# Second FFN of a hybrid block: load order on SP, places of the downward steps, loads of the last weights

## The chip, the cores and the metric

The kernel runs on one core of one Trainium2 chip. The metric is the device time of one execution in microseconds (us). Lower is better. Times before are the median of three runs, and the profile is of one more execution.

## The reference, cut to what matters

One block: a first feed-forward layer, a mixer of retention and sparse attention, a second feed-forward layer and a last norm, over 16 meta tokens and 512 real ones, in fp32. The change touches the second feed-forward layer, which here works on the 512 real tokens alone.

```python
D_MODEL, SEQ, D_FF = 1024, 512, 2816

def swiglu(u, w_gate, w_up, w_down):
    return (jax.nn.silu(u @ w_gate) * (u @ w_up)) @ w_down

# second FFN and the end of the block
h = h + 0.5 * swiglu(rmsnorm(h, ffn2_norm[l]), ffn2_w_gate[l], ffn2_w_up[l], ffn2_w_down[l])
y = rmsnorm(h, final_norm)
return y[:, N_META:]
```

## The kernel before

**Arithmetic.** Every fp32 operand is used as a high and a low part: ACT writes the high part of a weight (`whi`), DVE subtracts it from the raw weight to get the low part (`wlo`), and TensorE (PE) does three matmuls for each product. Now and then the two parts go into one spare buffer and are both called `wpair`.

**Units and steps.** The 2816 hidden columns are cut into six units: `u0` of 256 columns, `u1` to `u5` of 512. A unit from `u1` on is done by seven block products of tokens and gate or up weights, in the order `11`, `12`, `b`, `a`, `c`, `d`, `22` (`11`, `12`, `22` are blocks of the weights, `a` to `d` are sums of blocks). Each product is two steps, so a unit has upward steps 0 to 13; a step is 12 matmuls. They go to the PSUM banks X (tag `x`) and Z or Y (both tag `z`); in a profile these are `psqX`, `psqZ`, `psqY`, line 2489. Step 0 of the next unit begins bank X anew, so it waits until DVE has read the old X (`gated("A", ...)`, line 2352, `p<-psqX,RR,p`). Step 6 begins Y in the bank of Z, so it waits until DVE has added Z to the first copy (`add("A", "Z")`, line 2343, `p<-psqZ,p`, after step 3).

**The way of the hidden values.** After step 12 the second token half is gated, and after step 13 the first half. DVE transposes each in blocks (line 2359, `cross`), POOL writes them to DRAM in four DMAs (line 2362, `hts<-cross`), and SP fetches them back turned (line 2369, `land<-hts`; for `u0` the lines are 2552, 2555 and 2558). In the next unit ACT and DVE split them, with their block sums, into `hh`, `hl` and `he` (`turned_sums`; `hidden` for `u0` and for `u5`).

**Downward steps.** The product with `w_down` of units 1 to 4 is again seven block products, here called d0 to d6, one step of 12 matmuls each (`sums_down`, `psd`, line 2462). Their banks are reused: d4 may begin when DVE has taken d2 out of its bank, d5 after d3, d6 after d4 (`take`, line 2452, `hTok<-psd,hTok`). The steps of unit i - 1 are woven between the steps of unit i. Units 0 and 5 have plain downward steps (`down`, line 2660, 24 matmuls each).

**What sets the order.** `steps` is one list, and `steps_through` runs through it. At step i it first issues the load of step i + 4 (`pre`), then puts the `whi` of step i + 2 or i + 3 on ACT, then the matmuls of step i; half way through them come the `wlo` on DVE (`lower`) and all work put off to `late` (`catch_up`), and after them the step's posts (`posts_of`), among them `next_place`, which loads the next 1 MB upward weight into one of four places, in two DMAs. PE, ACT and DVE work through this in the written order, which `manual_schedule(engines=BUSY)` says. Up to step 13 of `u5` SP is not in that set: the framework's scheduler places its DMAs. From there to the end SP is in written order as well.

Of the kernel before, what the change touches and what calls it, by code (L numbers as in the profile page):

```python
# [18 lines left out]
P = 128  # L19
D = 1024  # L20
KD = D // P
S = 512
# [59 lines left out]
def kernel(ctx: ExitStack, tc: tile.TileContext, x, meta, g1, wg1, wu1, wd1, gm,  # L82
                      w_in, w_ro, w_ao, w_mo, g2, wg2, wu2, wd2, gf, rope, decay, causal, out):
    nc = tc.nc
    x, out = x[0], out[0]
# [3 lines left out]
    wg2, wu2, wd2 = wg2[0], wu2[0], wd2[0]  # L89
# [26 lines left out]
    def split(src, hi, lo, eng=nc.vector):  # L116
        nc.scalar.activation(hi, src, AF.Copy)  # L117
        eng.tensor_tensor(lo, src, hi.bitcast(F32), ALU.subtract)  # L118
# [11 lines left out]
    def load_w(src, nk, n):  # L130
        raw = wpool.tile([P, 2048], F32, tag="raw", name="raw", bufs=2)
        v = raw[:, : nk * n].rearrange("p (k c) -> p k c", k=nk)
        nc.sync.dma_start(v, src.rearrange("(k p) c -> p k c", p=P))
        return v

    def split_w(v, eng=nc.vector):
        nk, n = v.shape[1], v.shape[2]
        hi = wpool.tile([P, 1024 + WPAD], F32R, tag="whi", name="whi", bufs=3)[:, w_at[0] :]
        lo = wpool.tile([P, 1024 + WPAD], F32R, tag="wlo", name="wlo", bufs=3)[:, w_at[0] :]
        hv = hi[:, : nk * n].rearrange("p (k c) -> p k c", k=nk)  # L140
        lv = lo[:, : nk * n].rearrange("p (k c) -> p k c", k=nk)
        split(v, hv, lv, eng)
        return hv, lv
# [234 lines left out]
    BUSY = {mybir.EngineType.PE, mybir.EngineType.Activation, mybir.EngineType.DVE}  # L378
# [261 lines left out]
    if True:  # L640
# [226 lines left out]
        with tc.manual_schedule(engines=BUSY):  # L867
# [9 lines left out]
            raw = load_w(wg1[:, 2 * P : 4 * P], KD, 2 * P)  # L877
# [17 lines left out]
            raw = load_w(wu1[:, 2 * P : 4 * P], KD, 2 * P)  # L895
# [18 lines left out]
        def down(f0, nf, taken_by):  # L914

            raws = {}
            steps = []
            for c in range(KD):
                def pre(c=c):
                    if c % 2 == 0:  # L920
                        raws[c] = load_w(wd1[f0 * P : (f0 + nf) * P, c * P : (c + 2) * P], nf, 2 * P)

                def src(c=c):
                    return raws[c // 2 * 2][:, :, c % 2 * P : (c % 2 + 1) * P]

                def run(w, lower, c=c):
                    ps = [s1.bank("psd")[:, :TH] for _ in range(2)]
                    mm3([(ps[0], one), (ps[1], two)], w, lambda k: s1.hid[f0 + k], nf)
                    lower()
                    s1.catch_up()  # L930
                    for p_, sl in zip(ps, (one, two)):
                        nc.vector.scalar_tensor_tensor(hT[c][:, sl], p_, 0.5, hT[c][:, sl], ALU.mult, ALU.add)
                    taken_by(c)
                    s1.next_sum4()

                steps.append((pre, src, run))
            return steps
# [13 lines left out]
        steps = down(0, 4, keep_sums)  # L951
# [332 lines left out]
        units = [Values(0, OFF_RV), Values(1, OFF_RV + 2 * S), Values(2, OFF_AV)]  # L1284
# [185 lines left out]
    if True:  # L1470
# [418 lines left out]
        p = RH - 1  # L1889
# [69 lines left out]
        raw = vr["raw"]  # L1959
# [3 lines left out]
        for c in range(2):  # L1963
            t = rt.tile([P, S], F32, tag="sg", name="gate", bufs=4)
# [18 lines left out]
    with pool("ao") as ao:  # L1983
        vo = [ao.tile([P, AH, S], F32R, tag=f"vo{i}", name="vo") for i in range(2)]
        ao_parts = [(vo[0][:, c, :], vo[1][:, c, :]) for c in range(AH)]
        with pool("at") as at:
# [39 lines left out]
            def rope_k(ps, eng=nc.gpsimd):  # L2026
                y = rope_swap(ps, cos, sin, 64, T, eng)
                k = [at.tile([P, TX], F32R, tag=f"ak{i}", name="ak")[:, :T] for i in range(2)]
                split(y, k[0], k[1])
                return k  # L2030
# [103 lines left out]
            with tc.manual_schedule(engines=BUSY):  # L2134
                w = gr.next()
                k, q = rope_k(first_k, nc.vector), rope_q(first_q, nc.vector)
                t, t5 = (at.tile([P, S], F32, tag="gate", name="gate", bufs=2) for _ in range(2))
# [10 lines left out]
                raw = fetch_values(5, vraw())  # L2148
            pend = None
            for h in range(AH):  # L2150
# [9 lines left out]
                if more:  # L2160
                    q, k = proj_q(w if h == 0 else None), proj_k()
# [40 lines left out]
        steps = []  # L2202
# [4 lines left out]
        with pool("ou") as ou:  # L2207
# [6 lines left out]
            for c in range(KD):  # L2214
# [3 lines left out]
                if c < n_left:  # L2218
                    t = ou.tile([P, S], F32, tag="sa", name="sa", bufs=3)
                    nc.scalar.dma_start(t, gd[KD + c])  # L2220
                else:
                    t = sa[c - n_left]
# [20 lines left out]
    late, f2, fin = [], {}, {}  # L2243
# [31 lines left out]
    def new_place(name):  # L2275
        return places.tile([P, 4, S], F32, tag="w", name=name, bufs=4)
# [283 lines left out]
    units = [(Plain, Rows)[i > 0](i, f0, nf) for i, (f0, nf) in enumerate(UNITS)]  # L2560
# [192 lines left out]
    def posts_of(u):  # L2753

        i = u.i
        nxt = units[i + 1] if i + 1 < len(units) else None
        prev = units[i - 1] if i else None
        at = {j: [] for j in range(14)}

        def put(j, *do):  # L2760
            at[j] += do

        gate_of = lambda c, half: lambda: u.silu(c, half)
        if u is u0:
            put(0, lambda: split_t(1), lambda: new_t(2))
            put(1, lambda: split_t(2), lambda: new_t(3), lambda: squares(0))
            put(2, lambda: split_t(3), lambda: new_t(4), lambda: squares(1), lambda: squares(2), lambda: squares(3), token_norm)
            put(3, load_gf, lambda: split_t(4), u.gates, lambda: u1.wsum("b", 0), lambda: late.append(u.turned))
            return at
        put(1, lambda: u.copy("A", "p1", "X"))  # L2770
        put(2, lambda: put_off and put_off.pop()())
        put(3, lambda: u.add("A", "Z"), lambda: late.append(gate_of("A", 0)))
        if u.early:
            put(4, lambda: prev.new_hidden(hid_tile), lambda: late.append(prev.hidden(1)))
            put(6, lambda: late.append(prev.hidden(0)))
            put(1, lambda: u.wsum("b", 2))
            put(6, lambda: u.wsum("d", 0))
            put(7, lambda: u.wsum("d", 2))
        else:
            sums = []  # L2780
            put(2, lambda: sums.extend(prev.turned_sums()), lambda: sums[0]())
            put(4, lambda: sums[1]())
            put(5, lambda: sums[2]())
            put(6, lambda: sums[3]())
            put(8, lambda: sums[4]())
        put(5, lambda: u.copy("B", "u2", "X"))
        put(7, lambda: u.copy("C", "p5", "Y"))
        put(9, lambda: u.add("C", "X"))
        put(11, lambda: u.add("B", "Y"), lambda: late.append(gate_of("B", 1)))
        put(12, lambda: u.gated("C", u.room["C"], u.room["B"], 1), lambda: u.turn("C", "D", 1), lambda: u.fetch("C", 1))  # L2790
        put(13, lambda: u.gated("A", u.d["X"], u.room["A"], 0), lambda: late.append(turn_rest))
        for j in ((5, 7, 9, 11, 13) if u.early else range(1, 14, 2)):
            put(j, next_place)

        def turn_rest():
            u.turn("A", "B", 0)
            u.fetch("D", 0)

        return at
# [4 lines left out]
    def woven(i, places_):  # L2804

        for j, s in enumerate(wo[i]):
            steps.append(s)
            if j in places_:
                steps.append(places_[j])
# [11 lines left out]
    def halves_of_raw(i):  # L2821

        if not down_raw:
            t = wpool.tile([P, 2048], F32, tag="raw", name="raw", bufs=2).rearrange("p (h k c) -> p h k c", h=2, k=2)
            down_raw.extend(t[:, j] for j in range(2))
        down_raw.append(down_raw.pop(0))
        return down_raw[-1]

    for i in (2, 3, 4):
        woven(i, dict(zip(range(6, 13), units[i - 1].sums_down(halves_of_raw, {}))))  # L2830
    u4, u5 = units[4:]

    tail_w = []
# [4 lines left out]
        for low in lows:  # L2838
            low()

    tail_raw = []

    def load_tail():
        tail_raw.append(new_place("raw"))
        nc.sync.dma_start(tail_raw[0], wd2[u5.f0 * P : (u5.f0 + 4) * P, S:].rearrange("(k p) c -> p k c", p=P))

    def tail_weights():
        tail_w.extend(split_w(tail_raw[0][:, i : i + 2, :]) for i in (0, 2))

    ends = {}  # L2850

    def halves_of_place(i):
        if i < 3:
            return halves_of_raw(i)
        j = (i - 3) // 2
        if j not in ends:
            ends[j] = new_place("raw")
        return ends[j][:, (i - 3) % 2 * 2 :][:, :2]

    d = u4.sums_down(halves_of_place, {4: (load_tail,), 6: (last_halves,)})  # L2860
    woven(5, {7: d[0], 9: d[1], 11: d[2]})
    n_units = len(steps)
    c0, c1 = [], []
    steps += d[3:]
    steps.append(down(u5, 0, 0, c0, posts=(tail_weights,), rows=(2, 3, 0, 1), where=("x", "z")))
    steps.append(down(u5, 0, 2, c0, taken_by=finish))
    pair = []

    def other_parts(n, c):
# [5 lines left out]
    for i in range(lead_from + 3, n_units - 2, 4):  # L2875
        steps[i] = (*steps[i], other_parts)
        lead_to[:] = [i]
    with tc.manual_schedule(engines=BUSY):
        for _ in range(n_units):
            next(pipe)  # L2880
    f2["later"].close()
# [7 lines left out]
    with tc.manual_schedule(engines=BUSY | {mybir.EngineType.SP}):  # L2889
        c1 += [new_bank(t) for t in LAST]  # L2890
        ends = [(c1[b], wide) for b in range(3)] + [(c1[3][:, one], one)]
# [58 lines left out]
```

## Time and profile before

| | |
|---|---|
| median of 3 runs | 1526.95 us (1525.93 to 1526.99) |
| the profiled execution | 1525.19 us, its span 1523.4 us |
| mean granted TensorE clock | 0.988 |
| PE busy | 1485.2 us, 97% of the span |
| DVE, ACT, POOL busy | 1133.4, 733.8, 241.2 us |
| second FFN | from 1162.8 us (its first split in the chain) to the end |

How to read it: a 128x512 matmul that follows another starts 0.23 us after it, so a step of 12 takes 2.72 us, which is the beat of this stage. A time inside the stage is told from the span's start, or as T + so many us, where T is the end of the step 13 that is spoken of. A window's row gives each engine's busy time in that stretch, the granted clock of TensorE (1.00 is full), the busy share of the DMA engines and GB/s. A row of waits gives the engine and its line, what ended the wait, the sum, the count and the longest.

### The profile page before, as it was taken

Reading aid. Unit: us, or ns where it says so; the run is one execution under the profiler, and the core shown is the slowest. Engines: PE = TensorE matmul, PEld = TensorE weight load, DVE = VectorE, ACT = ScalarE, POOL = GpSimd, SP = SyncE. Lnnn points to the kernel's source line nnn. Section 1 sums busy time; section 2 is a strip of 40 time slices with the busy share of each in tenths; the row PEclk is TensorE's granted clock in tenths of the full one; section 3 lists DMA queues with packets and bytes.
Section 4 is the critical chain, followed back from the end, with each engine's and each line's share of the span. In section 5 each row is a group of like instructions: output and inputs, shape, how many; then the busy total and the mean of one; then the engine's idle time right before and its main releaser. Section 6 shows DMA issues by size and latency. Waiting matters only on the chain.

```text
span 1523.4 us, 22754 instructions
## 1 busy us (share of the span) xinstructions
PE 1485.2 (97%) x8800; PEld 1312.6 (86%) x8800; DVE 1133.4 (74%) x1747; ACT 733.8 (48%) x1052; POOL 241.2 (16%) x335
## 2 busy tenths in 40 slices
PE   9999999999999999999999999999999989999996
PEld 8999999999988888888888888988888777777775
DVE  4988585776887768778887878775567669678685
ACT  5555263454354444443333366775345444545443
POOL 1001010013221231212121323221012010010110
PEclk9999999999999999999999999999999999999998
DMA  5266566568776677676766645566474455666622
GB/s 168 78 184 164 152 172 166 151 169 251 244 211 205 194 202 210 165 215 143 212 156 164 172 115 165 156 195 194 133 265 139 158 184 202 202 210 203 218 91 103
DMA packets 198300, 269.78 MB, mean 177 GB/s; under 512 B 17328, under 2 KB 120904, under 8 KB 197552
## 3 DMA queue, kind: packets, MB, share of 16 engines
q1 hardware_dynamic: 171184, 207.89, 42.8%
q0 software_dynamic: 23904, 54.92, 16.3%
q10 hardware_dynamic: 3104, 5.53, 1.1%
q8 instruction: 69, 1.13, 0.3%
q14 instruction: 39, 0.32, 0.1%
HBM read 238.12 MB, written 80.49 MB: 209 GB/s over the span
## 4 chain that ended last, share of the span: by engine, by line
PE 88%; DVE 5%; DMA 3%; ACT 2%; issue 2%; POOL 0%; SPq 0%; ACTq 0%; POOLq 0%; DVEq 0%
PE psd L157 8%; PE psqX L157 7%; PE psrg L157 6%; PE psro L157 6%; PE psqX L2489 5%; PE psvX L1234 4%; PE psd L2462 4%; PE psqY L157 3%; PE psrk L157 3%; PE psqY L2489 3%; PE psrq L157 3%; PE psat L157 3%; PE psmo L157 3%; PE psak L157 3%; PE psaq L157 3%; PE psga L157 3%
## 5 line engine op out<-in xcount | busy, mean ns | idle before, releaser
L375 ACT ACTIVATE whi<-raw 128x1024 fp32r<-128x1024 f32 (+2 forms) x167 | 159.5, 957 | 132.2 <-PE psd L157 33.6
L376 DVE TENSOR_TENSOR wlo<-raw,whi 128x1024 fp32r<-128x1024 f32 (+2 forms) x167 | 187.7, 1127 | 46.2 <-ACT whi L375 46.1
L376 DVE TENSOR_TENSOR wlo<-w,whi 128x1024 fp32r<-128x1024 f32 x58 | 70.3, 1218 | 30.2 <-ACT whi L375 29.9
L375 ACT ACTIVATE whi<-w 128x1024 fp32r<-128x1024 f32 x58 | 61.2, 1057 | 51.5 <-PE psqY L2489 12.6
L157 PE MATMUL psro<-vo,whi 128*128 128x512 f32 x256 | 78.8, 389 | 0.0
L157 PE MATMUL psd<-hl,whi 128*128 128x264 f32 x352 | 71.4, 284 | 0.0
L157 PE MATMUL psd<-hh,wlo 128*128 128x264 f32 x352 | 70.8, 283 | 0.0
L117 ACT ACTIVATE whi<-raw 128x1024 fp32r<-128x1024 f32 (+1 forms) x44 | 45.4, 1036 | 52.4 <-PE psat L157 17.2
L157 PE MATMUL psd<-hh,whi 128*128 128x264 f32 x352 | 70.6, 282 | 0.0
L118 DVE TENSOR_TENSOR wlo<-raw,whi 128x1024 fp32r<-128x1024 f32 (+1 forms) x44 | 53.7, 1221 | 22.0 <-ACT whi L117 21.9
L2362 POOL DMA_DIRECT2D hts<-cross x40 | 25.7, 650 | 270.2 <-DVE cross L2359 269.9
L157 PE MATMUL psqX<-th,whi 128*128 128x264 f32 x216 | 61.1, 283 | 0.0
L157 PE MATMUL psqX<-tl,whi 128*128 128x264 f32 x216 | 61.1, 283 | 0.0
L157 PE MATMUL psqX<-th,wlo 128*128 128x264 f32 x216 | 61.1, 283 | 0.0
L157 PEld LDWEIGHTS psro<-vo,whi 128*128 128x128 f32 x256 | 48.1, 188 | 10.1 <-DVE vo L376 0.2
L157 PEld LDWEIGHTS psd<-hh,wlo 128*128 128x128 f32 x352 | 54.6, 188 | 0.0
L157 PEld LDWEIGHTS psd<-hh,whi 128*128 128x128 f32 x352 | 54.2, 188 | 0.0
L157 PEld LDWEIGHTS psd<-hl,whi 128*128 128x128 f32 x352 | 53.8, 188 | 0.0
L375 ACT ACTIVATE whi<-wsum 128x1024 fp32r<-128x1024 f32 x36 | 38.1, 1059 | 30.4 <-PE psd L157 14.9
L157 PE MATMUL psrg<-xh,whi 128*128 128x512 f32 x128 | 50.5, 394 | 0.0
L157 PE MATMUL psrg<-xl,whi 128*128 128x512 f32 x128 | 49.9, 390 | 0.0
L157 PE MATMUL psrg<-xh,wlo 128*128 128x512 f32 x128 | 49.9, 390 | 0.0
(622 smaller groups left out, 4822.9 us busy)
## 6 DMA issues: line engine op xcount, KB each, us to landing
raw<-in_w_in_dram SPq DMA_DIRECT2D x18, 1024.0 KB, 6.3
raw<-in_w_in_dram SPq DMA_DIRECT2D x33, 512.0 KB, 4.5
w<-in_w_in_dram SPq DMA_DIRECT2D x24, 512.0 KB, 6.0
raw<-in_ffn_w_up_dram SPq DMA_DIRECT2D x11, 1024.0 KB, 5.4
raw<-in_ffn_w_gate_dram SPq DMA_DIRECT2D x10, 1024.0 KB, 5.6
raw<-in_ffn_w_down_dram SPq DMA_DIRECT2D x20, 512.0 KB, 4.3
w<-in_ffn_w_gate_dram SPq DMA_DIRECT2D x20, 512.0 KB, 4.6
raw<-in_ffn_w_down_dram SPq DMA_DIRECT2D x12, 768.0 KB, 5.0
```

Of the source, the lines that this page charges most:

```text
L117: nc.scalar.activation(hi, src, AF.Copy)
L118: eng.tensor_tensor(lo, src, hi.bitcast(F32), ALU.subtract)
L157: nc.tensor.matmul(o, a[:, k, :], b[:, sl], start=first and k == 0 and i == 0, stop=last and k == nk - 1 and i == 2, skip_group_check=onto)
L375: nc.scalar.activation(hi, src, AF.Copy)
L376: return lambda: nc.vector.tensor_tensor(lo, src, hi.bitcast(F32), ALU.subtract)
L1234: nc.tensor.matmul(d[bank_][t], a, b[:, k, :], start=not onto and j + k + m == 0, stop=j + k == 3 and m == 2, skip_group_check=onto)
L2362: nc.gpsimd.dma_start(d.rearrange("(b i) a e -> a i b e", i=32)[a], cross[32 * a : 32 * a + 32].rearrange("p b c t -> p b (c t)"))
L2462: nc.tensor.matmul(ps[:, t], a, b[:, k, :], start=not onto and k + m == 0, stop=k == 1 and m == 2, skip_group_check=onto)
L2489: nc.tensor.matmul(ps[:, t], a, b[:, k, :], start=not onto and j + k + m == 0, stop=j + k == 3 and m == 2, skip_group_check=onto)
```

## The change

1. SP is added to the engines that keep the written order, for the whole of the list up to step 13 of `u5`.
2. The downward steps of units 1, 2 and 3 stand behind steps 7 to 13 of the unit after, where they stood behind 6 to 12.
3. In `u5`, two of unit 4's downward steps are woven (behind steps 7 and 10; it were three, behind 7, 9 and 11), and five instead of four stand behind step 13.
4. The last `w_down` weights (two loads of 1 MB, one for each half of the output columns) are loaded at steps 11 and 13 of `u5` into free places. Before, the first half came as two loads of 512 KB from `down`, and the second as one behind d4.
5. In `u1` the first token half of `u0` is split first (after step 4) and the second after step 6; it was the other way round. `u1` loads four weights ahead instead of five.

```diff
         if u.early:
-            put(4, lambda: prev.new_hidden(hid_tile), lambda: late.append(prev.hidden(1)))
-            put(6, lambda: late.append(prev.hidden(0)))
+            put(4, lambda: prev.new_hidden(hid_tile), lambda: late.append(prev.hidden(0)))
+            put(6, lambda: late.append(prev.hidden(1)))
...
-        for j in ((5, 7, 9, 11, 13) if u.early else range(1, 14, 2)):
+        for j in range(5 if u.early else 1, 12 if u.early else 14, 2):
             put(j, next_place)
+        if nxt is None:
+            put(11, lambda: load_last(0))
+            put(13, lambda: load_last(1))
...
     for i in (2, 3, 4):
-        woven(i, dict(zip(range(6, 13), units[i - 1].sums_down(halves_of_raw, {}))))
+        woven(i, dict(zip(range(7, 14), units[i - 1].sums_down(halves_of_raw, {}))))
...
+    def load_last(c):
+        t = last_raws[c] = new_place("raw")
+        nc.sync.dma_start(t, wd2[u5.f0 * P : (u5.f0 + 4) * P, c * S : (c + 1) * S].rearrange("(k p) c -> p k c", p=P))
...
-    d = u4.sums_down(halves_of_place, {4: (load_tail,), 6: (last_halves,)})
-    woven(5, {7: d[0], 9: d[1], 11: d[2]})
+    d = u4.sums_down(halves_of_place, {6: (last_halves,)})
+    woven(5, {7: d[0], 10: d[1]})
     n_units = len(steps)
     c0, c1 = [], []
-    steps += d[3:]
-    steps.append(down(u5, 0, 0, c0, posts=(tail_weights,), rows=(2, 3, 0, 1), where=("x", "z")))
-    steps.append(down(u5, 0, 2, c0, taken_by=finish))
+    steps += d[2:]
+    for k0 in (0, 2):
+        _, _, run, at_ = down(u5, 0, k0, c0, where=("x", "z"), **({"taken_by": finish} if k0 else {"posts": (tail_weights,), "rows": (2, 3, 0, 1)}))
+        steps.append((lambda: None, lambda k0=k0: last_raws[0][:, k0 : k0 + 2], run, at_))
...
-    with tc.manual_schedule(engines=BUSY):
+    with tc.manual_schedule(engines=BUSY | {mybir.EngineType.SP}):
         for _ in range(n_units):
             next(pipe)
```

**PE between step 13 of `u3` and step 0 of `u4`, before.** `psqX<-...,th` is step 13, `psqX<-...,xh` is step 0, which overwrites the same bank.

```order
L2489 MATMUL psqX<-whi,th 128x512
L2489 MATMUL psqX<-whi,tl 128x512
L2489 MATMUL psqX<-wlo,th 128x512
L2489 MATMUL psqX<-wpair,xh_11676 128x512
L2489 MATMUL psqX<-wpair,xl_11677 128x512
```

The same place now: `psd` is d6 of unit 2.

```order
L2489 MATMUL psqX<-whi,th 128x512
L2489 MATMUL psqX<-whi,tl 128x512
L2489 MATMUL psqX<-wlo,th 128x512
L2462 MATMUL psd<-whi,hh 128x512
L2462 MATMUL psd<-wlo,hh 128x512
```

A step of 12 matmuls on another bank has come between the last matmul into the old X and the first into the new one.

**SP around the same boundary, before.** `wa` to `wd` are upward weights of `u4`, `raw` those of downward steps, `land` the turned hidden values of `u3`. The two `raw` behind `wb` are the weights of d0 and d1 in `u4`.

```order
L2317 DMA wb<-usb_99 128x2x512 x2
L2431 DMA raw<-in_ffn_w_down_dram 128x2x512 x2
L2317 DMA wa<-usa_98 128x2x512 x2
L2317 DMA wc<-usc_100 128x2x512 x2
L2317 DMA wd<-usd_101 128x2x512 x2
L2369 DMA land<-hts 128x4x256
L2317 DMA w_13478<-in_ffn_w_up_dram 128x2x512 x2
L2369 DMA land<-hts 128x4x256
```

And now, where the first `raw` is that of d6 and the second that of d0:

```order
L2317 DMA wb<-usb_99 128x2x512 x2
L2431 DMA raw<-in_ffn_w_down_dram 128x2x512
L2369 DMA land<-hts 128x4x256
L2317 DMA wa<-usa_98 128x2x512 x2
L2369 DMA land<-hts 128x4x256
L2317 DMA wc<-usc_100 128x2x512 x2
L2317 DMA wd<-usd_101 128x2x512 x2
L2431 DMA raw<-in_ffn_w_down_dram 128x2x512
L2317 DMA w_13517<-in_ffn_w_up_dram 128x2x512 x2
```

Both fetches of hidden values have moved ahead of three weights, and the weight of d0 has moved behind both fetches.

**SP at the end of `u5`, before.** `dsb`, `dsa`, `dsc` and `dsd` are the weights of d2, d3, d4 and d5, the L2431 row without a letter that of d6; L2690 is the first half of the last weights and L2845 the second.

```order
L2431 DMA raw<-dsa_118 128x2x512
L2431 DMA raw<-dsc_120 128x2x512
L2431 DMA raw<-dsb_119 128x2x512
L2431 DMA raw<-dsd_121 128x2x512
L2431 DMA raw<-in_ffn_w_down_dram 128x2x512
L2690 DMA raw<-in_ffn_w_down_dram 128x2x512
L2369 DMA land<-hts 128x4x256 x2
L2690 DMA raw<-in_ffn_w_down_dram 128x2x512
L2845 DMA raw<-in_ffn_w_down_dram 128x4x512
```

And now, with L2848 for the last weights:

```order
L2431 DMA raw<-dsb_119 128x2x512
L2431 DMA raw<-dsa_118 128x2x512
L2431 DMA raw<-in_ffn_w_down_dram 128x2x512
L2848 DMA raw<-in_ffn_w_down_dram 128x4x512
L2431 DMA raw<-dsc_120 128x2x512
L2369 DMA land<-hts 128x4x256
L2431 DMA raw<-dsd_121 128x2x512
L2848 DMA raw<-in_ffn_w_down_dram 128x4x512
L2369 DMA land<-hts 128x4x256
```

Of the last weights only the second half still stands behind a fetch of hidden values; the weight of d5 (`dsd`) has moved behind the first of them.

More of the change, by code (lines that the diff above doesn't have):

```diff
@@ L2839, in last_halves @@
             low()
[L2841 to L2845, printed above, removed]
+    last_raws = {}
+    def load_last(c):
+        t = last_raws[c] = new_place("raw")
+        nc.sync.dma_start(t, wd2[u5.f0 * P : (u5.f0 + 4) * P, c * S : (c + 1) * S].rearrange("(k p) c -> p k c", p=P))
     def tail_weights():
-        tail_w.extend(split_w(tail_raw[0][:, i : i + 2, :]) for i in (0, 2))
+        tail_w.extend(split_w(last_raws[1][:, i : i + 2, :]) for i in (0, 2))
     ends = {}
     def halves_of_place(i):
-        if i < 3:
+        if i < 2:
             return halves_of_raw(i)
-        j = (i - 3) // 2
+        if i == 6:
+            return halves_of_raw(i)
+        j = (i - 2) // 2
         if j not in ends:
             ends[j] = new_place("raw")
-        return ends[j][:, (i - 3) % 2 * 2 :][:, :2]
-    d = u4.sums_down(halves_of_place, {4: (load_tail,), 6: (last_halves,)})
-    woven(5, {7: d[0], 9: d[1], 11: d[2]})
+        return ends[j][:, i % 2 * 2 :][:, :2]
+    d = u4.sums_down(halves_of_place, {6: (last_halves,)})
+    woven(5, {7: d[0], 10: d[1]})
     n_units = len(steps)
     c0, c1 = [], []
-    steps += d[3:]
-    steps.append(down(u5, 0, 0, c0, posts=(tail_weights,), rows=(2, 3, 0, 1), where=("x", "z")))
-    steps.append(down(u5, 0, 2, c0, taken_by=finish))
+    steps += d[2:]
+    for k0 in (0, 2):
+        _, _, run, at_ = down(u5, 0, k0, c0, where=("x", "z"), **({"taken_by": finish} if k0 else {"posts": (tail_weights,), "rows": (2, 3, 0, 1)}))
+        steps.append((lambda: None, lambda k0=k0: last_raws[0][:, k0 : k0 + 2], run, at_))
     pair = []
```

## The prediction

> **What bounds the kernel now.** I read the page first, then the waits of PE from 1150 us on, then the chain through that stretch, and last the rows of each engine around every wait of PE.
>
> ```profile
> PE 1485.2 (97%) x8800; PEld 1312.6 (86%) x8800; DVE 1133.4 (74%) x1747; ACT 733.8 (48%) x1052; POOL 241.2 (16%) x335
> ...
> PE psqX L2489 <- DVE p L2352: 9.9, 3, 3.3
> PE psd L2660 <- ACT hh L375: 5.7, 1, 5.7
> PE psqY L2489 <- DVE p L2343: 5.1, 1, 5.1
> PE psd L2462 <- DVE hTok L2452: 2.5, 1, 2.5
> PE psqX L2489 <- ACT u L2340: 2.4, 1, 2.4
> PE psd L2462 <- DVE hl L376: 2.0, 2, 1.2
> PE psd L2660 <- DVE hl L376: 1.3, 1, 1.3
> PE psqX L2489 <- DVE wlo L376: 0.3, 1, 0.3
> ```
>
> PE bounds the kernel, and the change takes no matmul away. So only PE's idle time in the second FFN can change: 29.2 us in these rows, and the slow matmuls behind the waits. The chain gives those:
>
> ```profile
> 1196.15 7.37 PE psqX L2489 x24
> 1246.70 5.42 PE psqY L2489 x12
> 1293.59 8.59 PE psqX L2489 x24
> 1421.78 7.34 PE psqX L2489 x24
> 1465.22 5.45 PE psqX L2489 x24
> ```
>
> The last row is the full beat: 24 matmuls in 5.45 us, 12 in 2.72. Behind waits they took more: 1.93 us (at 1196), 2.70 (1246), 3.15 (1293) and 1.90 (1421). At the boundary between, `u3` to `u4`, I count steps between two waits:
>
> ```profile
> 1358.30 0.77 PE L2489 MATMUL psqX<-wpair,xh 128*128 128x512 f32 x1 [3.31 <-DVE p L2352]
> 1380.55 0.50 PE L2462 MATMUL psd<-whi,hl 128*128 128x512 f32 x1 [1.15 <-DVE hl L376]
> ```
>
> From 1358.30 to 1379.40 stand seven steps and two matmuls, 19.50 us at the full beat, so 1.60 lost. Behind the 1.15 us wait nothing to speak of is lost.
>
> **u1, split order.** ACT's split of the second half of `u0` waited for a fetch that stood behind a weight on SP:
>
> ```profile
> 1182.33 0.37 SPq L2558 DMA_DIRECT2D land<-hts  x1
> 1187.85 0.88 SPq L2317 DMA_DIRECT2D w<-in_ffn_w_gate_dram  x2
> 1188.90 0.37 SPq L2558 DMA_DIRECT2D land<-hts  x1
> 1193.58 0.66 ACT L375 ACTIVATE hh<-land 128x512 fp32r<-128x512 f32 x1 [5.52 <-DMA land<-hts]
> ```
>
> Now that ACT row takes the first half, issued at 1182.33, and the second fetch stands ahead of the weight. The wait of 2.40 and its 1.93 us go: 4.3. The plain downward loads, moved behind that weight, start near 1189 for a step that begins about 1199 (1203.53 before, less 4.3); a load of that size lands within 5 us, so I cost them at nothing. Were that cover short, the downward step would wait.
>
> **u1 to u2.** Step 6 waits for `add("A", "Z")`, which stands on DVE behind `t`, which waits for a fetch behind a weight:
>
> ```profile
> 1234.02 0.89 SPq L2317 DMA_DIRECT2D w<-in_ffn_w_up_dram  x2
> 1235.09 0.92 SPq L2369 DMA_DIRECT2D land<-hts  x2
> 1233.91 3.63 DVE L2646 SCALAR_TENSOR_TENSOR hTok<-psd,hTok 128x128 f32<-128x128 f32 x16
> 1240.63 0.69 DVE L2401 TENSOR_TENSOR t<-land 128x512 f32<-128x512 f32 x1 [3.10 <-DMA land<-hts]
> 1245.34 1.22 DVE L2343 TENSOR_TENSOR p<-psqZ,p 128x1024 f32<-128x1024 f32 x1
> ```
>
> Now the fetch is ahead of three weights and `hTok` is late next: it ends at 1237.54. From `t`'s start to `p`'s end 5.93 us passed, so `p` would end at 1243.5 and step 6 start at 1243.6; PE is there at 1246.70 - 5.10 = 1241.6. About 2.0 us of the 5.10 stay. Behind them I take 1.0 us of slow matmuls (between nothing after 1.15 us and 1.93 after 2.40). Worth: 5.10 + 2.70 - 2.0 - 1.0 = 4.8; ends 3.9 and 7.8.
>
> **Three boundaries.** Old X is read by DVE after step 13; at 1355.00 (T, the end of step 13 of `u3`) DVE was not there yet:
>
> ```profile
> 1356.75 1.40 DVE L2352 SCALAR_TENSOR_TENSOR p<-psqX,RR,p 128x512 f32<-128x512 f32 x2
> ```
>
> The order of DVE's work is the same, so `p` still ends near T + 3.1, but PE now has d6, 2.72 us, in between. What stays is 3.31 - 2.72 = 0.6 us, too short for slow matmuls (the 1.15 us row). Worth: 3 x 2.72 + 3.15 + 1.60 + 1.90 = 14.8. If the slow matmuls came anyway, 8.2; if d6 itself had to wait, less.
>
> [...]
>
> **First downward step of u3, u4, u5.** The 2.0 us on `hl` go, since d0 is a step later and the first half's fetch no longer stands behind a weight. But the raw weight of d0 used to be loaded at 1338, far ahead, and now stands behind both fetches:
>
> ```profile
> 1338.34 5.81 SPq L2431 DMA_DIRECT2D raw<-in_ffn_w_down_dram  x2
> 1361.69 1.93 POOL L2362 DMA_DIRECT2D hts<-cross  x3 [0.25 <-issue]
> 1362.97 5.64 DMA hts<-cross
> raw<-dsb SPq DMA_DIRECT2D x4, 512.0 KB, 3.5
> GB/s 402 393 410 410 418 434 410 197 82 82 90 139 156 287 360 377 303 352 385 377 418 385 377 299 225 254 287 299 381 397 410 443 393 332 316 119 66 0 66 0
> 1200.00:1210.00 10.00, 10.00 (x44) 8.23 (x43) 6.95 (x7) 3.56 (x4) 0.00 (x0) 0.96 0.97 328
> 1250.00:1300.00 50.00, 46.69 (x190) 37.81 (x189) 39.81 (x47) 22.32 (x23) 5.14 (x8) 0.91 0.63 208
> ```
>
> The last write `hts` landed at 1368.61, T + 13.6. With the weights no longer in its way it may be 2.5 us after POOL's last issue, as at the end (1476.70 against 1474.23, below): T + 11.1. Then come fetch, two weights of 1 MB and the raw: 3.15 MB. At 410 GB/s (the full slices of 1422 to 1432 us) that is 7.7 us, and some 2.2 more for a load alone (3.5 - 1.3), so the raw is there at T + 21.0 to 23.5. Behind it lie `whi`, `wlo` and `hl`, 3.6 us; PE needs `hl` at T + 0.6 + 2.72 + 8 x 2.72 + 0.45 = T + 25.5. A wait of 0 to 1.6 us; I take 0.8, three times 2.4. In `u2` the writes are earlier against the steps; nothing. The same queue holds other weights: `wa` stands behind the first fetch (issued by T + 6) and is wanted at step 6 (T + 19.6), `wc` behind the second (by T + 14) for step 8 (T + 28); a 1 MB weight lands in about 5 us, so both are hidden by the steps between, and if not, `psq` rows would wait on `wlo`. Worth with the last row of PE's waits: 2.0 + 0.3 - 2.4 = -0.1; ends +2.3 and, at 328 GB/s (the mean of 1200 to 1210 us) and with 1.9 us of slow matmuls each, -14.
>
> **The end.** T is now 1470.67.
>
> ```profile
> 1470.06 1.30 DVE L2359 STREAM_TRANSPOSE cross<-p 128x512 f32<-128x512 f32 x2
> 1471.65 2.58 POOL L2362 DMA_DIRECT2D hts<-cross  x4 [44.81 <-DVE cross L2359]
> 1476.70 6.34 SPq L2369 DMA_DIRECT2D land<-hts  x2
> 1483.15 0.45 SPq L2690 DMA_DIRECT2D raw<-in_ffn_w_down_dram  x1
> 1487.83 1.06 ACT L375 ACTIVATE whi<-raw 128x1024 fp32r<-128x1024 f32 x1 [10.64 <-DMA raw<-in_ffn_w_down_dram]
> 1492.53 21.30 PE psd L2660 x82
> ```
>
> Here SP shows what a fetch does to a load behind it: the last weights, needed by ACT since 1477, start when the second fetch may, at 1483.15, and land 4.6 us later. That wait goes, but d5's weight now stands behind the first fetch. `cross` ended at T + 0.7, 5.4 us before that fetch; with no downward step between 11 and 13 it has one `take` (1.3 us) less ahead of it and ends near T - 0.5, so fetch and weight start at T + 4.9 and the weight, two issues later, lands at about T + 10. Then `whi` 1.06, `wlo` 1.22, and behind that `wlo` on DVE the `take` of d2, 1.28, each in its place with little between: T + 13.6. PE has finished d3 at T + 5.4 and cannot start d4: a new wait of some 8.2 us. Later d6 waits 0.9 and the first plain step 0.7 (`wlo` and `take`, 2.5 us, and `whi`, 1.06, do not fit into 2.72). Idle 9.8, slow matmuls 2.7 (as behind 5.10 us); before 2.48 + 5.70 + 1.34 = 9.5 and some 3.7 slow (the last row takes 21.30 us for 82 matmuls, 18.6 at the full beat, and about 1 is lost ahead of it). One step more behind step 13 costs nothing, it is one less ahead. Worth +0.7; between -3 (weight lands 3 us later) and +10.8 (weight in time: then 1.2 + 0.9 + 0.7 us of idle remain of 13.2).
>
> **Sum.** 4.3 + 4.8 + 14.8 - 0.1 + 0.7 = 24.5 us. 1525.19 - 24.5 = 1500.7 for an execution like the profiled one; the median of the runs lies 1.76 above that one, so 1502.5.
>
> **Rivals.**
> - The weight of d5 is in time, 10 us more: 1492. For it: a raw load alone takes 3.5 us. Against it: it would have to land by T + 3, and `cross`, on which its place on SP hangs, ends only at T - 0.5 with POOL and DRAM still to come.
> - The slow matmuls of the shorter waits belong to something else and come anyway. Then 1.93 + 6.65 us are not gained: 1511. For it: they are not in step with the waits (3.31 us cost 3.15, 1.60 and 1.90). Against it: 1.15 us cost none, and full beats run wherever PE does not wait. [...]
> - Slower: the fetches starve the woven steps. One place, SP at each boundary: everything for d0 and after it waits for the slower of two turns through DRAM. For it: 208 GB/s mean over 1250 to 1300 us; against it: the slices over 400 whenever loads are queued. At 208 the raw would land 7.4 us later than taken, and three boundaries would lose some 22 us and about 6 of slow matmuls: 1530. It turns slower where the 3.15 MB move below about 220 GB/s.
> - No change: the boundary waits only move to d6 (its `wlo` late) and the end loses 10 us: 1527. Against it: at T DVE has done that `wlo` a step earlier.
>
> **How the numbers follow.** Forecast with its own 1496 to 1508: 0.69. Weight of d5 in time: 0.05. Slow matmuls anyway: 0.07. Starved in part, 1508 to 1522: 0.11. Starved past the point: 0.05. No change: 0.03. Two runs of this kernel differ by up to 0.07%, and 0.2% (3 us) is what I count as a difference: faster 0.92, same 0.03, slower 0.05. The range takes in the early weight (1492) and the bad end of d0's wait (1502.5 + 14): 1491 to 1516, with about 0.05 left out on the slow side.
>
> **What would show it.** Right: no wait of step 0 on line 2352 over 1 us; step 6 of `u2` waits about 2 us; in `u1` no wait on line 2340; one wait of about 8 us of `psd` line 2462 on `hTok` behind step 13 of `u5`, with ACT's `whi` waiting for `raw<-dsd`. Wrong: waits of `psd` on `wlo` or `whi` of `raw` behind step 7 over 2 us, or DMA slices under 300 GB/s while weights are queued at a boundary.

## Result and the profile after

| | median | range | span of the profiled execution |
|---|---|---|---|
| before | 1526.44 us | 1525.50 to 1526.99 | 1523.4 us, clock 0.988 |
| after | 1513.25 us | 1511.19 to 1513.82 | 1510.9 us, clock 0.996 |

The change is faster: 0.9912 of the time before, 95% interval 0.9895 to 0.9929. That is 13.2 us, inside the range of the prediction (1491 to 1516) but outside the 1496 to 1508 that had most of the chances, and about half of the 24.5 us forecast. The first row below is from the page of the kernel after, the others are PE's waits from 1150 us on (engine and line, what ended the wait, sum in us, count, longest).

```profile
PE 1477.7 (98%) x8800; PEld 1304.3 (86%) x8800; DVE 1132.9 (75%) x1747; ACT 733.7 (49%) x1052; POOL 240.0 (16%) x335
...
PE psd L2462 <- DVE hTok L2452: 11.0, 2, 10.0
PE psqX L2489 <- ACT whi L375: 2.9, 3, 1.1
PE psqY L2489 <- DVE p L2343: 1.9, 1, 1.9
PE psqX L2489 <- DVE p L2352: 1.8, 3, 0.6
PE psqX L2489 <- DVE wlo L376: 1.6, 3, 0.5
PE psd L2462 <- DVE hl L376: 1.3, 2, 0.6
PE psqX L2489 <- ACT wpair L375: 1.0, 1, 1.0
PE psd L2462 <- DVE wpair L376: 0.8, 1, 0.8
PE psqX L2489 <- DVE wpair L376: 0.5, 1, 0.5
PE psd L2660 <- DVE hl L376: 0.3, 1, 0.3
```

The waits still sum to 23.1 us, against 29.2 before, so they give only 6.1 of the gain; the rest is that fewer matmuls run slowly behind waits (PE is busy 7.5 us less with the same matmuls). The boundary waits of `p` L2352 went from 9.9 to 1.8, and the wait on the copy `u` in `u1` is gone. New are the many short ones on `whi`, `wlo`, `wpair` and `hl`. In this table the first row runs from the span's start, and each of the next from the start of one unit's step 0 to the start of the next one's. Before, d2 of `u5` stood ahead of T; now it stands behind it, and the table counts it at its 2.72 us in the last row both times:

| stretch | before | after | gain | forecast |
|---|---|---|---|---|
| up to step 0 of `u3` | to 1293.59 | to 1283.43 | 10.2 | 11.8 |
| `u3` | 64.71 | 60.78 | 3.9 | 5.9 |
| `u4` | 63.48 | 62.56 | 0.9 | 4.3 |
| `u5` to T, without d2 | 46.17 | 47.39 | -1.2 | 1.9 |
| T to the last matmul, with d2 | 45.88 | 46.86 | -1.0 | 0.7 |

(The forecast's -0.1 for d0 is spread over the three stretches in the middle.) The gain thins out from unit to unit, and the end loses. The place where each of `u2` to `u5` loses most is step 8, shown here in `u3` (timeline of ACT, DVE and PE: start, duration, instruction, idle time ahead and what ended it):

```profile
1302.39 1.06 ACT L375 ACTIVATE whi<-raw 128x1024 fp32r<-128x1024 f32 x1 [1.74 <-DMA raw<-in_ffn_w_down_dram]
1306.48 1.12 ACT L375 ACTIVATE hh<-land 128x1024 fp32r<-128x1024 f32 x1 [3.03 <-DVE land L2410]
1307.50 1.01 ACT L2340 ACTIVATE u<-psqX 128x1024 f32<-128x1024 f32 x1
1308.41 1.05 ACT L375 ACTIVATE wpair<-wc 128x1024 fp32r<-128x1024 f32 x1
...
1303.48 1.23 DVE L376 TENSOR_TENSOR wlo<-raw,whi 128x1024 fp32r<-128x1024 f32 x1 [3.49 <-ACT whi L375]
1305.76 0.69 DVE L2410 SCALAR_TENSOR_TENSOR land<-land 128x512 f32<-128x512 f32 x1
...
1309.51 0.50 PE L2489 MATMUL psqX<-wpair,th 128*128 128x512 f32 x1 [1.05 <-ACT wpair L375]
1310.77 0.73 PE L2489 MATMUL psqX<-wpair,th 128*128 128x512 f32 x2 [0.53 <-DVE wpair L376]
```

Read it from the bottom: PE waits for ACT's `wpair<-wc`. ACT had no wait for that weight; it came late to it, because ahead of it stand the copy `u`, which frees bank X, and a split `hh` that waits 3.03 us for DVE's sum (line 2410). That sum stands on DVE behind the `wlo` and `hl` of d0, and they wait for d0's weight. The two waits (1.05 and 0.53 us) and two restarts (an estimated 0.28 us each, last section) cost about 2.1 us here, and about as much in each of the four units.

From the chain of waits (the chain that ended last, as in the prediction): steps 0 and 1 of `u5` behind the boundary, then the end, with the load of d5's weight, the matmuls behind PE's 10.04 us wait, and the last ones.

```profile
1406.77 5.72 PE psqX L2489 x24
...
1459.85 6.04 DMA raw<-dsd
...
1469.64 7.76 PE psd L2462 x24
...
1482.13 18.89 PE psd L2660 x82
```

24 matmuls take 5.44 us without a wait. Behind the boundary only 0.28 us are lost, at a granted clock of 1.00 (1406.77 to 1412.5), and behind the long wait 2.3 us are, at a clock of 0.50 (1469.6 to 1474).

### The profile page after: what moved, and what is told of

Its sections match the earlier page's. It is cut to its first block, busy times and chain, and to the rows that moved or that the text cites. A ratio compares the mean times of both kernels' runs of the same rounds, so it can differ in the third digit from the quotient of the medians.

```text
span 1510.9 us, 22745 instructions
## 1 busy us (share of the span) xinstructions
PE 1477.7 (98%) x8800; PEld 1304.3 (86%) x8800; DVE 1132.9 (75%) x1747; ACT 733.7 (49%) x1052; POOL 240.0 (16%) x335
## 4 chain that ended last, share of the span: by engine, by line
PE 87%; DVE 5%; DMA 3%; issue 2%; ACT 2%; SPq 0%; POOL 0%; ACTq 0%; DVEq 0%; POOLq 0%
PE psd L157 8%; PE psqX L157 7%; PE psrg L157 6%; PE psro L157 6%; PE psvX L1234 4%; PE psqX L2489 4%; PE psqY L157 3%; PE psrk L157 3%; PE psrq L157 3%; PE psga L157 3%; PE psat L157 3%; PE psmo L157 3%; PE psd L2462 3%; PE psak L157 3%; PE psaq L157 3%; PE psvY L1234 2%
## 5 line engine op out<-in xcount | busy, mean ns | idle before, releaser
L375 ACT ACTIVATE whi<-raw 128x1024 fp32r<-128x1024 f32 (+2 forms) x164 | 156.2, 955 | 135.1 <-PE psd L157 32.7
L376 DVE TENSOR_TENSOR wlo<-raw,whi 128x1024 fp32r<-128x1024 f32 (+2 forms) x164 | 184.0, 1125 | 48.1 <-ACT whi L375 48.0
L375 ACT ACTIVATE whi<-w 128x1024 fp32r<-128x1024 f32 x59 | 62.3, 1057 | 53.0 <-PE psd L2462 11.3
L117 ACT ACTIVATE whi<-raw 128x1024 fp32r<-128x1024 f32 (+1 forms) x44 | 45.4, 1037 | 50.3 <-PE psat L157 17.3
L375 ACT ACTIVATE whi<-wsum 128x1024 fp32r<-128x1024 f32 x36 | 38.1, 1059 | 30.4 <-PE psd L157 14.8
```

The costliest lines, as they stand in the source:

```text
L376: return lambda: nc.vector.tensor_tensor(lo, src, hi.bitcast(F32), ALU.subtract)
```

## Experiments

All times are medians; each ratio is to the kernel before on the same chip, with its 95% interval. Its median beside the runs was 1525.74 us (first four), 1525.44 (next four) and 1526.47 (last three). These differ by 1 us, so differences of that size between two experiments are not read.

**e1: d5's weight asked for with d4's** (from the changed kernel)

```diff
-        def sums_down(self, slots, posts):
+        def sums_down(self, slots, posts, ahead={}):
...
-                    d[i] = slots(i)
-                    self.down_load(d[i], n)
+                    for j in ahead.get(i, (i,)):
+                        d[j] = slots(j)
+                        self.down_load(d[j], self.ORDER[j][0])
...
-    d = u4.sums_down(halves_of_place, {6: (last_halves,)})
+    d = u4.sums_down(halves_of_place, {6: (last_halves,)}, {4: (4, 5), 5: ()})
```

> Edit: the changed kernel, with the weight of d5 asked for together with that of d4, one step earlier, so that on SP it stands ahead of the fetch of u5's hidden values. Theory A (the order on SP makes the wait at the end): the wait of d4 on the take of d2, 10.0 us in the changed kernel, falls to about 1 to 2 us, its 2.3 us of slow matmuls go, and the time falls by 8 to 11 us, to about 1503. Theory B (DVE is crowded there by gates, transposes and splits, and the take would be late anyway): the wait stays over 5 us and the time over 1508.

Measured: 1504.74 us (1504.22 to 1506.28), 0.9865 (0.9851 to 0.9879), 8.5 us less than the changed kernel. SP's timeline and PE's waits:

```profile
1444.62 0.46 SPq L2431 DMA_DIRECT2D raw<-dsd  x1
1461.93 0.36 SPq L2369 DMA_DIRECT2D land<-hts  x1
...
PE psd L2463 <- DVE hTok L2453: 2.9, 2, 2.0
```

The same 512 KB load now starts 17.3 us ahead of the fetch that it stood behind, and the wait falls from 10.0 to 2.0 us. So 8 of the 10 us at the end are a place in SP's row; 2.0 us stay here and in e6 to e8. The slow matmuls, which I had expected to go, did not in the profiled execution: 24 still take 7.35 us (7.76 in the changed kernel).

**e2: d0's weight asked for at the end of the unit before** (from the changed kernel)

```diff
+                if i == 0:
+                    first_down[self.i] = pre
+                    return (lambda: None, lambda: d[i], run, 0)
...
+        put(13, lambda: first_down.pop(u.i, lambda: None)())
```

> Edit: the changed kernel, with the weight of d0 of each unit asked for after step 13 of the unit before, ahead of the second fetch and of two upward weights on SP. Theory A (the waits around step 8 of u2 to u5, some 9 us in rows of PE's waits with a little lost at each restart, come from d0's weight, behind which ACT and DVE hold the copy that frees bank X and the weight of step 8): they fall to under 3 us and the time falls by 6 to 9 us, to about 1506. Theory B (the chain of splits and block sums on ACT and DVE after the second fetch sets these waits): less than 3 us, 1511 or more.

Measured: 1509.12 us (1508.66 to 1509.58), 0.9892 (0.9878 to 0.9906), 4.1 us less than the changed kernel. SP now asks for it between the two fetches; and the first of PE's waits at step 8 of `u3`:

```profile
1285.07 0.46 SPq L2431 DMA_DIRECT2D raw<-in_ffn_w_down_dram  x1
1293.72 0.36 SPq L2369 DMA_DIRECT2D land<-hts  x1
...
1309.20 0.50 PE L2492 MATMUL psqX<-wpair,th 128*128 128x512 f32 x1 [0.81 <-ACT wpair L375]
```

The waits of d0 itself (`hl`, `wpair` of L2462) are gone. Step 8 still waits 0.8 and 0.5 us in four units. The gain lies between those of the two theories (6 to 9 us, and less than 3). So d0's weight was part of the cause. What stays may be the order of work on ACT and DVE; e7 and e8 test that.

**e3: the changed kernel with SP left to the scheduler**

```diff
-    with tc.manual_schedule(engines=BUSY | {mybir.EngineType.SP}):
+    with tc.manual_schedule(engines=BUSY):
```

> Edit: the changed kernel without SP in the written order up to step 13 of u5; all else stays. Theory A (written order on SP gains at u1 to u2 and loses at d0 and at the end): the wait at step 6 of u2 comes back (about 5 us and slow matmuls, 6 us in all), the waits around step 8 and the long one at the end go (about 20 us with slow matmuls), the time is about 1500. Theory B (written order on SP is what pays): the time is above 1515.

**e4: the kernel before with the weaving alone**

```diff
-        woven(i, dict(zip(range(6, 13), units[i - 1].sums_down(halves_of_raw, {}))))
+        woven(i, dict(zip(range(7, 14), units[i - 1].sums_down(halves_of_raw, {}))))
```

> Edit: the kernel before with one part of the change alone, the downward steps of units 1 to 3 behind steps 7 to 13. Theory A (each boundary of two of these three units, u2 to u3, u3 to u4, u4 to u5, loses 2.7 us of idle time and its slow matmuls, and the two waits on hl go): 14.8 + 2.0 less, about 1510. Theory B (the boundary wait only moves elsewhere, because DVE has the same work): within 4 us of before, 1522 or more.

Measured: e3 1516.74 us (1515.16 to 1519.78), 0.9943 (0.9930 to 0.9956); e4 1529.98 us (1527.11 to 1530.88), 1.0024 (1.0015 to 1.0034), a little slower than before. PE's longest row of waits in e3:

```profile
PE psqY L2489 <- DVE p L2343: 19.8, 4, 5.2
```

and in e4, with SP's timeline and one piece of the chain:

```profile
PE psqY L2489 <- DVE p L2343: 19.7, 4, 5.8
...
1299.83 0.37 SPq L2317 DMA_DIRECT2D w<-in_ffn_w_up_dram  x1
1300.39 1.25 SPq L2369 DMA_DIRECT2D land<-hts  x1
1301.69 0.50 SPq L2317 DMA_DIRECT2D w<-in_ffn_w_up_dram  x1
...
1313.19 8.55 PE psqY L2489 x24
```

In both, the boundary waits are 0.6 us, as in the changed kernel. But now step 6 waits about 5 us in all four units, where before it did so in `u2` alone. The weaving does not do this directly: the scheduler, which places SP's DMAs here, has placed them in another order. In `u3` of the kernel before, the first fetch stood ahead of the upward weight:

```profile
1296.37 0.36 SPq L2369 DMA_DIRECT2D land<-hts  x1
1305.47 0.89 SPq L2317 DMA_DIRECT2D w<-in_ffn_w_up_dram  x2
```

In e4 it stands behind the first half of that weight, which by the chain waited for a split of DVE that ended at 1299.82. So the fetch goes out at T + 12.9 us instead of T + 6.1, and `p` (line 2343) ends at T + 25.5 instead of T + 21.0. That is 4.5 of the 5.8 us that step 6 waits in `u3`; for the rest PE is earlier at step 6, since no matmuls run slowly behind the boundary (24 take 5.74 us there, 8.59 before). Behind the wait they are slow again (8.55 us for 24). So e4 changes SP's order along with the weaving, and no run has the new weaving with the fetches where they stood before. What e3 and e4 show is that the gain of the boundaries is lost again at step 6 when the fetch comes that late; the changed kernel, where it is early, keeps it.

Of e3 I had expected that the waits around step 8 and the long one at the end go, and they did (2.0 us at the end). I had expected the wait of step 6 to come back in `u2` alone, and about 1500 us: that was missed, and the time is that of theory B.

**e5: the kernel before with SP in written order, nothing else**

```diff
-    with tc.manual_schedule(engines=BUSY):
+    with tc.manual_schedule(engines=BUSY | {mybir.EngineType.SP}):
```

> The kernel before with SP's row kept in written order, and nothing else: the instructions of the four other engines stay in their order. Theory A (each part gains where I put it): the fetches of the two halves stand ahead of the weights, so the 5.1 us wait at step 6 of u2 and its 2.7 us fall to about 2, the 2.4 us of u1 mostly go, the three boundary waits of 3.3 us stay: 10 to 13 us gained, 1513 to 1516. Rival (the parts only work together, as the change of the weaving alone gained nothing): the fetches were early enough behind the boundary waits, only u1 to u2 gains, and the loads of the downward weights, now behind fetches, give part of it back: 1520 to 1526.

Measured: 1564.70 us (1563.11 to 1565.54), 1.0257 (1.0242 to 1.0272): 39 us slower than before, which neither theory had. PE's waits, then SP (with its row of waits from 1235 to 1270 us), ACT and PE at one of the seven waits:

```profile
PE psd L2462 <- DVE hTok L2452: 34.1, 7, 10.2
...
1255.96 0.88 SPq L2317 DMA_DIRECT2D w<-in_ffn_w_gate_dram  x2
1256.93 0.42 SPq L2431 DMA_DIRECT2D raw<-dsa  x1
...
SPq L2317 <- DVE wlo L376: 20.6, 2, 10.9
...
1262.32 1.06 ACT L375 ACTIVATE whi<-raw 128x1024 fp32r<-128x1024 f32 x1 [8.90 <-DMA raw<-dsa]
...
1265.98 0.77 PE L2462 MATMUL psd<-whi,hh 128*128 128x512 f32 x1 [5.05 <-DVE hTok L2452]
```

The gate weight is asked for early, but its place is still in use: SP stands up to 10.9 us at such a weight, until DVE has split what was there. `dsa`, written behind it, goes out directly after it, and so does `dsc`. ACT then waits 8.90 us for `dsa`, and PE 5.05 us. What had been predicted does come (no wait on the copy `u` in `u1`, and 1.9 us in place of 5.1 at step 6), but 34.1 us of waits on downward weights come with it.

**e9: weaving and SP's order; e10: SP's order and one call of `next_place` fewer in `u1`** (both from the kernel before). e9 is e5 with the diff of e4, e10 is e5 with

```diff
-        for j in ((5, 7, 9, 11, 13) if u.early else range(1, 14, 2)):
+        for j in range(5 if u.early else 1, 12 if u.early else 14, 2):
```

> The kernel before with two parts: SP in written order and the downward steps behind steps 7 to 13. Not taken over is the third one, a single call of next_place fewer in u1, after which each upward weight of u2 to u5 is asked for one place later. Theory A (the shift of next_place is what keeps the downward weights from standing behind a gate weight that waits for its place): boundary waits are 0.6, but dsb or dsa and dsd stay late, some 3 to 5 us twice a unit in three units with slow matmuls behind them, as with SP alone: 1535 to 1555. Rival (the place in the weaving is what counts): no such waits, the end with its 10 us wait as in the changed kernel: 1513 to 1518.

> The kernel before with SP in written order and one call of next_place fewer in u1; the downward steps stay behind steps 6 to 12. Theory A: the downward weights dsa and dsd are in time again; what stays are the boundary waits of 3.3 to 3.9 us with slow matmuls (14.8 us in three) and the end with d5's weight 10 us late. Against SP alone some 35 us come back: 1522 to 1530. Rival (the shift is nothing by itself): waits on hTok as with SP alone, 1550 or more.

Measured: e9 1579.11 us (1578.70 to 1581.55), 1.0351 (1.0337 to 1.0365); e10 1526.70 us (1524.61 to 1530.33), 1.0005 (0.9996 to 1.0015). The longest row of waits in e9:

```profile
PE psd L2462 <- DVE hTok L2452: 55.0, 10, 10.4
```

and in e10, with SP:

```profile
PE psd L2462 <- DVE hTok L2452: 10.4, 1, 10.4
...
1250.48 0.37 SPq L2431 DMA_DIRECT2D raw<-dsa  x1
```

With one call fewer each upward weight stands one place later in the row. In e10 `dsa` goes out at 1250.48, where in e5 it stood until 1256.93, and of the seven waits on `hTok` one is left, that at the end. The line is worth 38 us on top of SP's order (1564.70 to 1526.70), and without it the weaving makes things worse: 55.0 us of these waits in e9, whose time lies 24 us above the 1535 to 1555 of theory A, and whose boundary waits are still 2.7 to 3.0 us where I had expected 0.6. The order on SP and the place of `next_place` are one change, not two.

**e11: the changed kernel with `u0`'s halves split in the order of before**

```diff
-            put(4, lambda: prev.new_hidden(hid_tile), lambda: late.append(prev.hidden(0)))
-            put(6, lambda: late.append(prev.hidden(1)))
+            put(4, lambda: prev.new_hidden(hid_tile), lambda: late.append(prev.hidden(1)))
+            put(6, lambda: late.append(prev.hidden(0)))
```

> The changed kernel with the splits of u0's two halves in the order of before (second half first). Theory A (SP's order alone puts the second fetch ahead of the weight, so the second half lands about when ACT asks for it): the same time as the changed kernel, 1512.5 to 1514.5, ACT's hh at most 1 us later than its 1188.3, no wait of PE in u1. Rival (the order of the splits is what gained in u1, as I wrote): a wait on the copy u in u1 again, 2.4 us and its slow matmuls, 1516 to 1518.

Measured: 1514.10 us (1510.74 to 1516.55), 0.9925 (0.9912 to 0.9939), the changed kernel's time within the spread. ACT's row for the second half:

```profile
1188.34 0.66 ACT L375 ACTIVATE hh<-land 128x512 fp32r<-128x512 f32 x1 [0.30 <-DMA land<-hts]
```

It waits 0.30 us, where it waited 5.52 before, and PE has no wait in `u1`. So SP's order alone gives this gain (e5 has it too). But the order of the splits alone gives it as well. In e3 the second fetch still stands behind the weight, the first half is split first, ACT's split has no wait, and PE has none in `u1`:

```profile
1188.30 0.88 SPq L2317 DMA_DIRECT2D w<-in_ffn_w_gate_dram  x2
1189.35 0.37 SPq L2558 DMA_DIRECT2D land<-hts  x1
...
1188.42 0.65 ACT L375 ACTIVATE hh<-land 128x512 fp32r<-128x512 f32 x1
```

Where one of the two is there, the other brings nothing that can be measured.

**e6, e7, e8: towards a faster kernel.** e6 is e1 and e2 together. e7 is e6 with the copy `u` of units 2 to 5 ahead of DVE's sum and its split (the old place of the copy then holds for `u1` alone); e8 is e7 with that sum a step later (the marks `# e7` and `# e8` are not in the code):

```diff
             put(4, lambda: sums[1]())
-            put(5, lambda: sums[2]())
-            put(6, lambda: sums[3]())
+            put(5, lambda: u.copy("B", "u2", "X"), lambda: sums[2]())   # e7
+            put(6, lambda: sums[3]())
...
-            put(5, lambda: u.copy("B", "u2", "X"), lambda: sums[2]())
-            put(6, lambda: sums[3]())
+            put(5, lambda: u.copy("B", "u2", "X"))                      # e8
+            put(6, lambda: sums[2](), lambda: sums[3]())
```

> The changed kernel with both early loads: d5's weight asked for with d4's, and the first downward weight of each unit at the end of the unit before. If the two places are independent, 8.5 and 4.1 us add: 1513.25 - 12.6 = 1500.6, with the end wait at 2 us and step 8 still waiting 0.8 + 0.5 us in four units. If moving d0's load gives part back at the end (another load in the queue ahead of d4's and d5's), 1503 or more.

> As the kernel with both early loads, and the copy that frees bank X for step 8 stands on ACT ahead of the split hh that waits for DVE's sum. Theory A (the 0.8 us wait of step 8 is that copy and the split of the weight behind it, on ACT): copy and split come 1 us earlier, the 0.8 us wait and its restart go in four units, 4 us less than both early: 1496.5. Rival (DVE's chain sets step 8 too, since hl and the low half of the weight stand there): the wait moves to wlo, 0.5 becomes 1.0 or more, and 1 us or less is gained.

> As the kernel with the copy first, and the sum and its split (line 2410, hh, hl) a step later, behind the split of the weight for step 8. Theory A: neither engine has anything waiting ahead of that weight any more, both waits of step 8 (0.8 and 0.5 us, each with about 0.27 us to restart) go in four units: 7 to 8 us less than both early, 1493. Rival (hl, now a step later, is late for the third downward step, or the copy itself ends late): a new wait at that step, 1496 or more.

Measured: e6 1500.06 us (1499.86 to 1501.17), 0.9835 (0.9821 to 0.9849); e7 1495.77 us (1494.72 to 1497.15), 0.9807 (0.9792 to 0.9821); e8 1495.56 us (1495.44 to 1496.79), 0.9806 (0.9792 to 0.9820). In e6 PE waits 0.81 and 0.53 us at step 8 of `u3`.

ACT, and PE at the same step, in e7:

```profile
1302.67 1.00 ACT L2340 ACTIVATE u<-psqX 128x1024 f32<-128x1024 f32 x1
...
1309.18 0.73 PE L2493 MATMUL psqX<-wpair,th 128*128 128x512 f32 x2 [0.52 <-DVE wpair L376]
```

and in `u3` of e8 PE's only wait of that size behind the boundary, which is in step 9:

```profile
1314.25 0.50 PE L2493 MATMUL psqX<-wlo,th 128*128 128x512 f32 x1 [0.53 <-DVE wlo L376]
```

The two early loads add up (12.6 expected, 13.2 measured). In e7 the copy runs while ACT had stood idle, the 0.8 us waits are gone in all four units, and 4.3 us come, as theory A had it. In e8 the 0.5 us wait is gone from step 8 too, but one of the same size stands in step 9, on the next `wlo`, behind work that came later with the sum: its 1493 was missed, and the time is about the rival's 1496, though the wait is not at the step that the rival named. e7 and e8 are the same within the spread, 17.5 us better than the changed kernel.

## Why the prediction was right and wrong

- **`u1`, 4.3 us: right in size.** I gave two reasons as if both were needed. e11 shows that the fetch ahead of the weight does it alone, and e3 that the order of the splits does.
- **`u1` to `u2`, 4.8 us: right, a little low.** The wait that stays is 1.91 us (I had 2.0), and the 1.0 us of slow matmuls behind it did not come (the granted clock was 1.00 from 1239.5 to 1243 us).
- **Boundaries, 14.8 us: right as a term.** Three waits of 0.59 us, and 24 matmuls behind them take 5.72 us. But I wrote it as the weaving's worth. It also needs the fetch to be early: e4, with the weaving and the scheduler's SP, loses 4.2 us, since the fetch comes 6.8 us later and step 6 waits for it.
- **d0, -0.1: the step that failed.** For d0 itself I had three waits of 0.8 us, and 2.0 us came in all. The step "`wc` for step 8 ... hidden by the steps between" followed the weight through the DMA queue and stopped there. I did not follow ACT's row behind d0's split: `hh` waiting for DVE, then the copy that frees X, then the weight of step 8. This took 6.1 us in eight waits, and an estimated 2.2 us in eight restarts (0.28 us each, last section). The loads themselves came as forecast: d0's weight in `u3` landed at T + 22.2, between the 21.0 and 23.5 of the prediction.
- **The end, +0.7: right in kind, too small.** The wait was forecast with its cause and place; it is 10.0 us instead of 8.2, and 1.4 of the 1.8 are d5's load, which took 6.04 us and not 4.6. Three waits sum to 11.3 us against 9.8, and the end lost 1.0. (The upper end of this term, +10.8, should be 10.4 by its own figures, 13.2 less 1.2, 0.9 and 0.7.) No run takes parts 3 and 4 of the change alone. From T to the last matmul, with d2, it takes 45.9 us before, 37.0 in e3 (these parts, SP free), 47.6 in e10 (SP's order without them) and 46.9 with both. By these runs the new end is worth about 9 us with SP free, and SP's order takes them away.
- **What no term had.** One line, four weights ahead in `u1` instead of five, was in my description of the change and had no price. e5 and e10 put it at 38 us. It cost the sum nothing only because the change has it; had it been missing, my account would still have said 1502. I asked what each load waits for, and not what waits behind a load whose place is not yet free.
- **Rivals.** The time measured is near that of the rival with slow matmuls that come anyway (1511), but not for its reason: no matmuls are slow behind the boundaries. d5's weight in time was given 10 us, and e1 shows 8.5. The time falls into the band that I gave to starved fetches (1508 to 1522, chance 0.11), but nothing starved: at the boundary into `u3` the queue moved 381 to 409 GB/s from 1294 to 1304 us. That the time lies in the stated range is luck in part, since the range reached that far for late loads with slow matmuls behind them, and those did not come.

## What to carry to other kernels

With SP's loads in written order, each stood behind the slowest buffer ahead of it (up to 10.9 us in e5). So go down the queue, and for each load whose buffer is still in use list what stands behind it (here one call of a loader moved decided over 38 us). Where a scheduler places the loads, an edit to another engine can move them: compare its row in both kernels before you credit the edit (in e4 a fetch moved by 6.8 us). When a load comes late, follow the whole row of each engine that serves the step, not its operand alone. The parts of such a change could not be priced one by one and added here.

## What was not expected of the hardware

Waits of the same length did not cost the same. Behind the 1.98 us wait at the end, 24 matmuls took 7.35 us in e1 and 5.71 in e8, against 5.44 without a wait. A window behind that wait (engine busy times with counts, then the granted clock, DMA share, GB/s), in e1:

```profile
1463.60:1466.00 2.40, 2.39 (x6) 1.92 (x7) 2.19 (x3) 0.00 (x0) 0.41 (x1) 0.53 0.82 260
```

and in e8:

```profile
1454.50:1457.00 2.50, 2.50 (x11) 2.10 (x12) 2.16 (x3) 0.00 (x0) 0.40 (x1) 1.00 0.88 277
```

The granted clock was 0.53 in the one and 1.00 in the other. The length of the wait does not explain it, since it was 1.98 us both times, and no run here shows what does.

Short waits close together cost clock in e1 and none in the changed kernel. In `u5` of e1 PE waits 0.76, 0.64, 1.03 and 0.52 us within 7 us (d0 and step 8). The 22 matmuls behind them, and a window among them:

```profile
1435.69 6.90 PE psqX L2490 x22
...
1438.00:1440.00 2.00, 2.00 (x6) 1.55 (x6) 1.02 (x2) 2.00 (x3) 0.00 (x0) 0.54 0.08 15
```

In the changed kernel, with 0.64, 1.05 and 0.53 us at the same place, 22 matmuls take 5.43 us, at a granted clock of 1.00 (1435.13 to 1440.56). The 1.5 us lost in e1, where the clock was 0.54, are as much as the profiled execution of e1, 1506.28 us, lies above the median of its four. The lone waits of 0.59 us at the boundaries cost no clock: it was 1.00 over the 5.72 us behind each of the three.

What these waits cost even so is a restart: behind the 0.59 us of a boundary 24 matmuls take 5.72 us against 5.44, so 0.28 us that the row of waits does not hold. With eleven short waits in `u2` to `u5` of the changed kernel that is, by estimate, some 3 us.
